# Residual kept in the output, four of eight quads by seven products, one ordinary quad's low parts made by a transfer

## The chip, the cores and the metric

The kernel runs on one core of one Trainium2 chip. The time is the device time of one execution in microseconds; the times shown are medians of several runs. A core has TensorE (PE, matrix products, results in PSUM), VectorE (DVE), ScalarE (ACT), GpSimd (POOL) and SyncE (SP), which here only issues transfers. Each engine works through its own list of instructions in order and waits on semaphores for the others; a transfer is issued by an engine's queue and moved by the core's 16 DMA engines.

## The reference

One transformer layer for 256 tokens of width 2048 in float32. The first half mixes tokens by two attention branches and ends in a projection that is added to the residual x. The second half, where the change lies, is a gated feed-forward network with 5632 hidden columns:

```python
x = x + (g[:, :, 0] * y_a + g[:, :, 1] * y_b) @ w_o
gt, up = jnp.split(rms_norm(x, g_ffn) @ w_gate_up, 2, axis=-1)
return x + (jax.nn.silu(gt) * up) @ w_down
```

## The kernel before, in words

**Three products for one.** float32 operands are split into a high part (rounded to the type fp32r, by ScalarE) and a low part (the operand minus the high part, by VectorE). A product is then three matmuls into the same PSUM bank, high x high, high x low, low x high (`mm3`, L427 to L429). So every weight that is loaded passes through ScalarE (`split_pair`, L220, "wh") and VectorE (L221, "wl") before TensorE can use it.

**The feed-forward stage.** The hidden columns come in 11 blocks of 512, grouped in five parts of 3, 2, 2, 2 and 2 blocks (`PARTS`). For each block there is a gate-up group, which makes 512 columns of gate and 512 of up over all 16 slices of 128 rows of the normalised x. When the blocks of a part are done, their down projection follows, four groups of 512 output columns, two and two interleaved, in chunks of four slices. `evac_down` (L701) then adds a group's PSUM result to the residual `x1[j]` in SBUF on VectorE (L703); after the last part the sum goes out.

**Quads.** A gate-up group consists of eight quads (`Quad`), each a 2 x 2 block product: two token halves, two row slices, gate and up. An ordinary quad does it in 8 block products, 24 matmuls. The quads in `FAST` use a scheme of seven products (21 matmuls), which needs sums of weight blocks: `split_fast` (L837) splits three raw blocks (rh and rl for two, r for one), makes four sums in place in the loaded tile x with four dependent VectorE additions (L844 to L847), and `split` (L850) then splits the four results (wh, wl). The activations get such sums too (`job_h`: hP for an ordinary quad, hs/hsh/hsl for one in `FAST`), once. Ordinary quads add into banks C and D, those in `FAST` into A and B first, then into C and D; `evac_fast` (L658) and `evac_pair` combine the banks on VectorE and ScalarE after the group, and its result is transposed during the next group (tile hid).

**Order and buffers.** SyncE issues the loads; a load needs one of three tiles x (pool `xp`), which is released by the last split that reads it. wh and wl lie in a pool of six (three chunks), the raw parts and all activations in a pool `tp` of 28 tiles of 4 KB per partition. In the feed-forward stage a scheduler of the framework sets the order on each engine from priorities and its own cost model; the order is fixed when the program is built. Chunks are numbered through the program: 253 to 260 are the eight quads of the first gate-up group of part 1, 261 to 268 those of its second, and the tiles of a chunk bear its number (wl255, x257).

Of the kernel before, what the change touches and what calls it, by code (L numbers as in the profile page):

```python
# [41 lines left out]
NPAIR = KD // 2  # L42
FAST = (2, 4, 6)

# [51 lines left out]
def layer_kernel(ctx: ExitStack, tc: tile.TileContext, a: dict, out: bass.AP):  # L96
# [540 lines left out]
    def evac_wo(j):  # L637
        def evac(ps, step):
# [3 lines left out]
            for t in range(NT):  # L642
                nc.scalar.activation(sq[:, t], x1[j][:, t], AF.Square, accum_out=ss2[:, t, j:j + 1])

            for i in (2 * j, 2 * j + 1):
                hjobs[i] = Job(job_h(i))
                hjobs[i].ready = step + 2
                jobs.append(hjobs[i])
# [52 lines left out]
    def evac_down(half, j):  # L701
        def evac(ps, step):
            nc.vector.tensor_add(x1[j], ps, x1[j])  # L703
            if half == len(PARTS) - 1:
                nc.sync.dma_start(od[:, :, j * 512:(j + 1) * 512], x1[j])
        return evac

    def evac_last(ps, t):
# [109 lines left out]
    early = {}  # L818

    def load(c):  # L820
        g, gi, ks, q = chunks[c]
        t = xt[c] = xp.tile([P, 4, 512], F32, name=f"x{c}", tag="x")
        if q:
            for kk in range(2):
                src = g.w[(2 * q.i + kk) * P:(2 * q.i + kk + 1) * P].rearrange("p (n f) -> p n f", n=2)
                nc.sync.dma_start(t[:, 2 * kk:2 * kk + 2], src[:, :, g.c0:g.c0 + 512])
            return
# [9 lines left out]
    def split_fast(c):  # L837
# [10 lines left out]
        raws[c] = {1: (r[:, 0], r[:, 1]), 3: (rh[:, 0], rl[:, 0]), 2: (rh[:, 1], rl[:, 1])}  # L848

    def split(c):  # L850
        g, gi, ks, q = chunks[c]
        if q and q.fast and c not in raws:
            split_fast(c)
# [5 lines left out]
        if q and q.fast:  # L859
            parts[c] = raws.pop(c) | {m: (h[:, n], l[:, n]) for n, m in enumerate((7, 5, 6, 4))}  # L860
        else:
            parts[c] = (h, l)

# [8 lines left out]
    def products_quad(c):  # L872
        q = chunks[c][3]
        bank, w = held["q"], parts.pop(c)
        if not q.fast:
            h, l = w
            for t, n in ((1, 0), (0, 0), (0, 1), (1, 1)):
                m = PLAIN[t, n]
                for kk in range(2):
                    s = slice(t * P, (t + 1) * P)  # L880
                    mm3(bank[m], hP[q.i][:, 0, kk, s], hP[q.i][:, 1, kk, s], h[:, 2 * kk + n], l[:, 2 * kk + n],
                        q.first and kk == 0, q.last and kk == 1)
# [60 lines left out]
    for j in range(4):  # L943
        at(gidx("evac_g0", j), lambda j=j: load_bias(j))
        at(gidx("evac_g1", j), lambda j=j: load_bias(4 + j))
        at(gidx("evac_wo", j), lambda j=j: load_xres(j))

    after_evac = {}
    after_evac[gidx("evac_b", 0)] = lambda: jobs.append(prep["kr"])
# [10 lines left out]
    def splits(to):  # L960

        while ahead["split"] < min(to, n):
            c = ahead["split"]
            loads(c + 1)
            if c + 1 < n and chunks[c + 1][3] and chunks[c + 1][3].fast and c + 1 not in raws:
                loads(c + 2)
                split_fast(c + 1)
            split(c)
            ahead["split"] += 1
# [90 lines left out]
```

## Time and profile before

| | |
|---|---|
| median of 3 runs | 1356.28 us (1355.2 to 1356.44) |
| profiled execution, its own time | 1356.11 us |
| its span in the trace | 1354.3 us |
| TensorE busy | 1339.5 us (99%), clock granted 1.0 |
| VectorE, ScalarE, GpSimd busy | 949.1, 652.2, 34.3 us |
| moved by DMA | 257.14 MB, mean 190 GB/s |
| GpSimd's queue | 224 packets, 0.01 MB |

The page's busy share is an average over stages with different work, so it is read together with the stretches of one gate-up group or one down projection. A row of the timeline has the start, the duration, the engine, the line, the operation with its output and inputs, and in brackets the idle time before it and what ended that. Matmuls overlap: their rate is the distance from start to start.

### The profile page before, as it was taken

The page shows a single profiled execution, that of the slowest core. Times are in us where ns is not written, and L with a number is a line of the kernel's source. Part 1 is how long each engine was busy: PE and PEld are TensorE (multiplying, and loading weights), DVE is VectorE, ACT ScalarE, POOL GpSimd, SP SyncE. Part 2 cuts the span into 40 slices and gives each one's busy share as a digit, 9 for nine tenths or more (in the row PEclk, how much of TensorE's full clock was granted, in tenths as well). Part 3 has the DMA queues.
Part 4 walks back from the last instruction along what each step waited for, and adds up shares of the span by engine and source line. Part 5 has one row for each costly group of instructions (what it writes and reads, how often), then busy time and mean ns, then how long its engine had stood idle before and what let it go on. Part 6 is the DMA issues. An engine that isn't in the chain of part 4 may idle for free.

```text
span 1354.3 us, 16169 instructions
## 1 busy us (share of the span) xinstructions
PE 1339.5 (99%) x6243; PEld 1126.0 (83%) x6243; DVE 949.1 (70%) x949; ACT 652.2 (48%) x724; POOL 34.3 (3%) x41
## 2 busy tenths in 40 slices
PE   8999999999999999999999999999999999999998
PEld 6899999988888888888788888888878888888886
DVE  5566777677645655567789756886798579857973
ACT  6455555454444444455455434454445345534541
POOL 1011112000000000000000000000000000000000
PEclk9999999999999999999999999999999999999999
DMA  7555555656556766676546665565457654754662
GB/s 247 179 175 161 161 170 167 184 161 176 174 186 205 212 188 202 209 235 207 201 158 213 221 187 183 191 213 190 157 185 245 191 186 172 229 190 163 214 214 93
DMA packets 138205, 257.14 MB, mean 190 GB/s; under 512 B 9192, under 2 KB 28688, under 8 KB 138128
## 3 DMA queue, kind: packets, MB, share of 16 engines
q1 hardware_dynamic: 137760, 255.96, 58.9%
q8 instruction: 49, 0.80, 0.2%
q14 instruction: 28, 0.23, 0.1%
q10 hardware_dynamic: 144, 0.13, 0.0%
q0 software_dynamic: 224, 0.01, 0.0%
HBM read 253.97 MB, written 2.10 MB: 189 GB/s over the span
## 4 chain that ended last, share of the span: by engine, by line
PE 94%; DVE 2%; issue 1%; DMA 1%; ACT 1%; SPq 0%; DVEq 0%; ACTq 0%
PE g L429 14%; PE g L427 14%; PE g L428 13%; PE sC L427 6%; PE sC L429 6%; PE sC L428 6%; PE mA L427 4%; PE mA L429 4%; PE mA L428 4%; PE sD L429 4%; PE sD L427 4%; PE sD L428 4%; PE mB L428 3%; PE mB L429 3%; PE mB L427 3%
## 5 line engine op out<-in xcount | busy, mean ns | idle before, releaser
L220 ACT CAST wh<-x 128x1024 fp32r<-128x1024 f32 (+3 forms) x349 | 465.3, 1352 | 437.0 <-DVE x L847 127.7
L221 DVE TENSOR_TENSOR wl<-x,wh 128x2048 fp32r<-128x2048 f32 x132 | 300.8, 2289 | 134.5 <-ACT wh L220 132.7
L221 DVE TENSOR_TENSOR wh<-x,wh 128x1024 fp32r<-128x1024 f32 (+2 forms) x217 | 250.6, 1172 | 113.1 <-ACT wh L220 111.9
L427 PE MATMUL g<-wh,xTh 128*128 128x512 f32 (+1 forms) x544 | 210.6, 387 | 0.6 <-ACT xTh L212 0.6
L429 PE MATMUL g<-wh,xTl 128*128 128x512 f32 (+1 forms) x544 | 207.9, 382 | 0.6 <-DVE xTl L217 0.6
L428 PE MATMUL g<-wh,xTh 128*128 128x512 f32 (+1 forms) x544 | 207.9, 382 | 0.0
L429 PEld LDWEIGHTS g<-wh,xTl 128*128 128x128 f32 x544 | 102.8, 189 | 17.6 <-DVE xTl L217 1.4
L427 PEld LDWEIGHTS g<-wh,xTh 128*128 128x128 f32 x544 | 102.8, 189 | 15.9 <-ACT xTh L212 0.9
L428 PEld LDWEIGHTS g<-wh,xTh 128*128 128x128 f32 x544 | 102.9, 189 | 15.4 <-DVE wh L221 0.4
L427 PE MATMUL sC<-wh,hP 128*128 128x512 f32 x220 | 86.1, 391 | 1.6 <-DVE u L679 1.5
L429 PE MATMUL sC<-wh,hP 128*128 128x512 f32 x220 | 85.7, 390 | 0.0
L429 PE MATMUL sD<-wh,hP 128*128 128x512 f32 x220 | 85.7, 389 | 0.0
L428 PE MATMUL sC<-wl,hP 128*128 128x512 f32 x220 | 85.7, 389 | 0.0
L427 PE MATMUL sD<-wh,hP 128*128 128x512 f32 x220 | 85.7, 389 | 0.0
L428 PE MATMUL sD<-wl,hP 128*128 128x512 f32 x220 | 85.7, 389 | 0.0
L220 ACT CAST rh<-x 128x1024 fp32r<-128x1024 f32 x33 | 34.7, 1051 | 36.1 <-DMA x<-in_w_gate_up_dram 36.1
L427 PEld LDWEIGHTS sC<-wh,hP 128*128 128x128 f32 x220 | 41.3, 188 | 12.3 <-issue 4.0
L427 PE MATMUL g<-wh,mTh 128*128 128x512 f32 x128 | 50.5, 394 | 0.0
L429 PE MATMUL g<-wh,mTl 128*128 128x512 f32 x128 | 49.9, 390 | 0.0
L428 PE MATMUL g<-wh,mTh 128*128 128x512 f32 x128 | 49.9, 390 | 0.0
L427 PEld LDWEIGHTS sD<-wh,hP 128*128 128x128 f32 x220 | 41.3, 188 | 8.6
L428 PEld LDWEIGHTS sD<-wl,hP 128*128 128x128 f32 x220 | 41.3, 188 | 8.6
(675 smaller groups left out, 2390.7 us busy)
## 6 DMA issues: line engine op xcount, KB each, us to landing
x<-in_w_gate_up_dram SPq DMA_DIRECT2D x176, 512.0 KB, 4.7
x<-in_w_down_dram SPq DMA_DIRECT2D x88, 512.0 KB, 5.0
x<-in_w_in_dram SPq DMA_DIRECT2D x79, 512.0 KB, 4.2
x<-in_w_in_dram SPq DMA_DIRECT2D x56, 448.0 KB, 3.6
x<-in_w_o_dram SPq DMA_DIRECT2D x32, 512.0 KB, 4.4
x<-in_w_o_mla_dram SPq DMA_DIRECT2D x16, 512.0 KB, 4.9
x<-in_w_o_dil_dram SPq DMA_DIRECT2D x16, 512.0 KB, 4.6
x<-in_w_ukv_dram SPq DMA_DIRECT2D x8, 512.0 KB, 4.0
```

Source lines behind the costliest of these rows:

```text
L220: nc.scalar.copy(h, x)
L221: nc.vector.tensor_sub(l, x, f32(h))
L427: nc.tensor.matmul(ps, ah, bh, start=first, stop=False)
L428: nc.tensor.matmul(ps, ah, bl, start=False, stop=False)
L429: nc.tensor.matmul(ps, al, bh, start=False, stop=last)
```

## The change

There are three edits.

1. `FAST` becomes (2, 4, 5, 6): quad 5 of each of the 11 gate-up groups is done with seven products.
2. Quad 3 (`BY_DMA`) stays an ordinary quad, but its low parts are no longer made by VectorE. ScalarE writes minus the rounded weights into l and the rounded weights into h, and GpSimd's queue loads the same weights from memory once more with an adding transfer, so that l becomes weight minus high part (`split_by_dma`). This is called two chunks ahead (`EARLY`) and uses four tiles of `tp` in place of a wh and a wl.
3. The residual is written to the output when it is made, and its SBUF tiles are free from then on. After each part but the last ScalarE copies the PSUM result to a tile y and GpSimd's queue adds it to the output in memory; for the last part the output is loaded back (`load_x1`) and the sum is made as before.

```diff
--- before.py
+++ after.py
@@ -40,7 +40,9 @@
 PARTS = ((0, 3), (3, 5), (5, 7), (7, 9), (9, 11))
 PRIO = 200
 NPAIR = KD // 2
-FAST = (2, 4, 6)
+FAST = (2, 4, 5, 6, )
+BY_DMA = (3,)
+EARLY = 2
 
 
 class Job:
@@ -642,6 +644,7 @@
             for t in range(NT):
                 nc.scalar.activation(sq[:, t], x1[j][:, t], AF.Square, accum_out=ss2[:, t, j:j + 1])
 
+            nc.sync.dma_start(od[:, :, j * 512:(j + 1) * 512], x1[j])
             for i in (2 * j, 2 * j + 1):
                 hjobs[i] = Job(job_h(i))
                 hjobs[i].ready = step + 2
@@ -700,10 +703,19 @@
 
     def evac_down(half, j):
         def evac(ps, step):
-            nc.vector.tensor_add(x1[j], ps, x1[j])
-            if half == len(PARTS) - 1:
-                nc.sync.dma_start(od[:, :, j * 512:(j + 1) * 512], x1[j])
+            cols = od[:, :, j * 512:(j + 1) * 512]
+            if half < len(PARTS) - 1:
+                y = t4([P, NT, 512], f"y{half}_{j}")
+                nc.scalar.copy(y, ps)
+                nc.gpsimd.dma_start(cols, y, accum_op=ALU.add)
+            else:
+                nc.vector.tensor_add(x1[j], ps, x1[j])
+                nc.sync.dma_start(cols, x1[j])
         return evac
+
+    def load_x1(j):
+        x1[j] = t4([P, NT, 512], f"x1b_{j}")
+        nc.sync.dma_start(x1[j], od[:, :, j * 512:(j + 1) * 512])
 
     def evac_last(ps, t):
         for c in range(t + 1):
@@ -817,13 +829,17 @@
         first_step.setdefault(chunks[c][1], i)
     early = {}
 
+    def quad_src(c, kk):
+        g, gi, ks, q = chunks[c]
+        src = g.w[(2 * q.i + kk) * P:(2 * q.i + kk + 1) * P].rearrange("p (n f) -> p n f", n=2)
+        return src[:, :, g.c0:g.c0 + 512]
+
     def load(c):
         g, gi, ks, q = chunks[c]
         t = xt[c] = xp.tile([P, 4, 512], F32, name=f"x{c}", tag="x")
         if q:
             for kk in range(2):
-                src = g.w[(2 * q.i + kk) * P:(2 * q.i + kk + 1) * P].rearrange("p (n f) -> p n f", n=2)
-                nc.sync.dma_start(t[:, 2 * kk:2 * kk + 2], src[:, :, g.c0:g.c0 + 512])
+                nc.sync.dma_start(t[:, 2 * kk:2 * kk + 2], quad_src(c, kk))
             return
         if gi == 0 and c:
             load_x(ks[0] * P, (ks[-1] + 1) * P)
@@ -847,8 +863,21 @@
         add(x[:, 3], x[:, 2], x[:, 3])
         raws[c] = {1: (r[:, 0], r[:, 1]), 3: (rh[:, 0], rl[:, 0]), 2: (rh[:, 1], rl[:, 1])}
 
+    def split_by_dma(c):
+
+        x = xt.pop(c)
+        h, l = ([t4([P, 2, 512], f"{n}{k}_{c}", F32R) for k in range(2)] for n in "hl")
+        for k in range(2):
+            nc.scalar.activation(l[k], x[:, 2 * k:2 * k + 2], AF.Copy, scale=-1.0)
+            nc.scalar.copy(h[k], x[:, 2 * k:2 * k + 2])
+            nc.gpsimd.dma_start(l[k], quad_src(c, k), accum_op=ALU.add)
+        parts[c] = [z[k][:, n] for z in (h, l) for k in range(2) for n in range(2)]
+        parts[c] = parts[c][:4], parts[c][4:]
+
     def split(c):
         g, gi, ks, q = chunks[c]
+        if c in parts:
+            return
         if q and q.fast and c not in raws:
             split_fast(c)
         t = xt.pop(c)
@@ -859,7 +888,7 @@
         if q and q.fast:
             parts[c] = raws.pop(c) | {m: (h[:, n], l[:, n]) for n, m in enumerate((7, 5, 6, 4))}
         else:
-            parts[c] = (h, l)
+            parts[c] = ([h[:, n] for n in range(4)], [l[:, n] for n in range(4)]) if q else (h, l)
 
     def needs_of(i):
         c, ks, _, _ = steps[i]
@@ -878,7 +907,7 @@
                 m = PLAIN[t, n]
                 for kk in range(2):
                     s = slice(t * P, (t + 1) * P)
-                    mm3(bank[m], hP[q.i][:, 0, kk, s], hP[q.i][:, 1, kk, s], h[:, 2 * kk + n], l[:, 2 * kk + n],
+                    mm3(bank[m], hP[q.i][:, 0, kk, s], hP[q.i][:, 1, kk, s], h[2 * kk + n], l[2 * kk + n],
                         q.first and kk == 0, q.last and kk == 1)
         else:
             h, l = hq[q.i]
@@ -945,6 +974,9 @@
         at(gidx("evac_g1", j), lambda j=j: load_bias(4 + j))
         at(gidx("evac_wo", j), lambda j=j: load_xres(j))
 
+    for j in range(4):
+        at(gidx("evac_down", 4 * (len(PARTS) - 1) + j), lambda j=j: load_x1(j), 2)
+
     after_evac = {}
     after_evac[gidx("evac_b", 0)] = lambda: jobs.append(prep["kr"])
     after_evac[gidx("evac_b", 6)] = lambda: limited.extend(attn["dil", p] for p in range(4))
@@ -965,6 +997,10 @@
             if c + 1 < n and chunks[c + 1][3] and chunks[c + 1][3].fast and c + 1 not in raws:
                 loads(c + 2)
                 split_fast(c + 1)
+            e = c + EARLY
+            if e < n and chunks[e][3] and chunks[e][3].i in BY_DMA and e not in parts:
+                loads(e + 1)
+                split_by_dma(e)
             split(c)
             ahead["split"] += 1
```

How the scheduler's order changes is shown at three places of part 1. First VectorE in the first group, from the low part of its first quad in `FAST` (255) on. Before:

```order
L221 TENSOR_TENSOR wl255_6410<-x255_6338,wh255_6409 128x2048
L221 TENSOR_TENSOR rl257_6441<-x257_6413,rh257_6440 128x1024
L221 TENSOR_TENSOR r257_6442<-x257_6413,r257_6442 128x512
L221 TENSOR_TENSOR wl256_6452<-x256_6381,wh256_6451 128x2048
L844 TENSOR_TENSOR x257_6413<-x257_6413 128x512
L845 TENSOR_TENSOR x257_6413<-x257_6413 128x512
L846 TENSOR_TENSOR x257_6413<-x257_6413 128x512
L847 TENSOR_TENSOR x257_6413<-x257_6413 128x512
L221 TENSOR_TENSOR wl257_6483<-x257_6413,wh257_6482 128x2048
L221 TENSOR_TENSOR wl258_6522<-x258_6455,wh258_6521 128x2048
L221 TENSOR_TENSOR rl259_6511<-x259_6486,rh259_6510 128x1024
```

And with the change:

```order
L223 TENSOR_TENSOR wl255_6480<-x255_6394,wh255_6479 128x2048
L223 TENSOR_TENSOR rl257_6511<-x257_6483,rh257_6510 128x1024
L223 TENSOR_TENSOR r257_6512<-x257_6483,r257_6512 128x512
L223 TENSOR_TENSOR rl258_6549<-x258_6521,rh258_6548 128x1024
L860 TENSOR_TENSOR x257_6483<-x257_6483 128x512
L223 TENSOR_TENSOR r258_6550<-x258_6521,r258_6550 128x512
L861 TENSOR_TENSOR x257_6483<-x257_6483 128x512
L860 TENSOR_TENSOR x258_6521<-x258_6521 128x512
L862 TENSOR_TENSOR x257_6483<-x257_6483 128x512
L861 TENSOR_TENSOR x258_6521<-x258_6521 128x512
L863 TENSOR_TENSOR x257_6483<-x257_6483 128x512
L862 TENSOR_TENSOR x258_6521<-x258_6521 128x512
```

The raw parts and sums of 257 and 258 (quads 4 and 5) now alternate, and the next rows are rl259, the last sum of 258 and wl257; quad 3 (256) no longer stands in the list.

Second, ScalarE at the same place. Before:

```order
L220 CAST rh255_6366<-x255_6338 128x1024
L220 CAST r255_6368<-x255_6338 128x512
L220 CAST wh254_6377<-x254_6307 128x2048
L220 CAST wh255_6409<-x255_6338 128x2048
L220 CAST rh257_6440<-x257_6413 128x1024
L220 CAST wh256_6451<-x256_6381 128x2048
```

And with the change:

```order
L222 CAST rh255_6424<-x255_6394 128x1024
L222 CAST r255_6426<-x255_6394 128x512
L871 ACTIVATE l0_256_6440<-x256_6435 128x1024
L872 CAST h0_256_6438<-x256_6435 128x1024
L871 ACTIVATE l1_256_6441<-x256_6435 128x1024
L872 CAST h1_256_6439<-x256_6435 128x1024
L709 COPY y0_3_6476<-mA_5135 128x1024
L222 CAST wh255_6479<-x255_6394 128x2048
L222 CAST rh257_6510<-x257_6483 128x1024
L222 CAST r257_6512<-x257_6483 128x512
L222 CAST rh258_6548<-x258_6521 128x1024
L222 CAST r258_6550<-x258_6521 128x512
```

The four operations of quad 3 and a copy of the down projection's result now stand ahead of wh255.

Third, VectorE in the second group, after the low part of its first quad in `FAST` (263). Before:

```order
L221 TENSOR_TENSOR wl263_6697<-x263_6615,wh263_6696 128x2048
L847 TENSOR_TENSOR x265_6700<-x265_6700 128x512
L221 TENSOR_TENSOR wl264_6739<-x264_6661,wh264_6738 128x2048
L215 TENSOR_TENSOR hid1l0_6778<-mA_5115,hid1h0_6777 128x1024
L221 TENSOR_TENSOR wl265_6782<-x265_6700,wh265_6781 128x2048
L221 TENSOR_TENSOR wl266_6821<-x266_6742,wh266_6820 128x2048
L221 TENSOR_TENSOR rl267_6810<-x267_6785,rh267_6809 128x1024
L221 TENSOR_TENSOR r267_6811<-x267_6785,r267_6811 128x512
```

And with the change, a few rows behind wl263 (three sums of 265 stand between):

```order
L217 TENSOR_TENSOR hid1l0_6858<-mA_5135,hid1h0_6857 128x1024
L223 TENSOR_TENSOR rl266_6862<-x266_6822,rh266_6861 128x1024
L223 TENSOR_TENSOR wl265_6873<-x265_6784,wh265_6872 128x2048
L223 TENSOR_TENSOR r266_6863<-x266_6822,r266_6863 128x512
L223 TENSOR_TENSOR rl267_6901<-x267_6876,rh267_6900 128x1024
L860 TENSOR_TENSOR x266_6822<-x266_6822 128x512
L223 TENSOR_TENSOR r267_6902<-x267_6876,r267_6902 128x512
L861 TENSOR_TENSOR x266_6822<-x266_6822 128x512
L860 TENSOR_TENSOR x267_6876<-x267_6876 128x512
L862 TENSOR_TENSOR x266_6822<-x266_6822 128x512
L861 TENSOR_TENSOR x267_6876<-x267_6876 128x512
L863 TENSOR_TENSOR x266_6822<-x266_6822 128x512
```

Two more sums of 267 and then wl266 and wl267 follow. Between wl263 and wl266 there are now two sets of raw parts and their sums. The tile x266 is the one that quad 3 (264) had: its load waits for ScalarE, as SyncE's rows with their waits show (a chunk is two rows; names with HW are earlier loads).

```order
L842 DMA x264_6731<-in_w_gate_up_dram 128x2x512 [waits DMAHW1_49,DMAHW0_49,DVE_49]
L842 DMA x264_6731<-in_w_gate_up_dram 128x2x512
L842 DMA x265_6784<-in_w_gate_up_dram 128x2x512 [waits DMAHW3_49,DMAHW2_49,DVE_49]
L842 DMA x265_6784<-in_w_gate_up_dram 128x2x512
L842 DMA x266_6822<-in_w_gate_up_dram 128x2x512 [waits DMAHW7_49,DMAHW6_49,Activation_49]
L842 DMA x266_6822<-in_w_gate_up_dram 128x2x512
L842 DMA x267_6876<-in_w_gate_up_dram 128x2x512 [waits DMAHW5_49,DMAHW4_49,DVE_49]
L842 DMA x267_6876<-in_w_gate_up_dram 128x2x512
```

The wait on Activation in x266's first row is for the operations of quad 3; the others wait for VectorE.

## Prediction

> **What bounds the kernel now.** I read the page's busy lines first, then the chain that ended last, then the stages one by one.
>
> ```profile
> span 1354.3 us, 16169 instructions
> PE 1339.5 (99%) x6243; PEld 1126.0 (83%) x6243; DVE 949.1 (70%) x949; ACT 652.2 (48%) x724; POOL 34.3 (3%) x41
> PE 94%; DVE 2%; issue 1%; DMA 1%; ACT 1%; SPq 0%; DVEq 0%; ACTq 0%
> ```
>
> TensorE sets the time: it is busy throughout and holds 94% of the chain. A matmul less is time less, if nothing else makes TensorE wait. What a matmul is worth is its distance to the next one, not its 0.39 us, which overlap. Here are the first and last of 18 matmuls in a row of an ordinary quad, and the first of the next group.
>
> ```profile
> 867.91 0.39 PE L427 MATMUL sC<-wh,hP 128*128 128x512 f32 x1
> ...
> 871.77 0.39 PE L429 MATMUL sD<-wh,hP 128*128 128x512 f32 x1
> 872.31 0.47 PE L427 MATMUL sC<-wh,hP 128*128 128x512 f32 x1 [0.16 <-DVE u L679]
> ```
>
> (871.77 - 867.91) / 17 = 0.227 us. An ordinary quad (24 matmuls) takes 5.45 us, one by seven products (21) 4.77 us. The engine that could take TensorE's place is VectorE. Part 1 in three stretches (gate-up group, gate-up group, down; the columns are TensorE, its weight loads, VectorE, ScalarE, GpSimd, each with a count, then clock, DMA share and GB/s):
>
> ```profile
> 829.60:872.30 42.70, 42.56 (x188) 34.94 (x187) 34.89 (x33) 20.16 (x15) 0.00 (x0) 1.00 0.58 197
> 872.30:915.20 42.90, 42.89 (x193) 35.45 (x194) 37.16 (x35) 20.90 (x17) 0.00 (x0) 1.00 0.59 196
> 915.20:959.00 43.80, 42.84 (x194) 35.33 (x193) 27.67 (x21) 19.01 (x13) 0.00 (x0) 1.00 0.59 192
> ```
>
> The 70% of the page is an average: 82% and 87% in the two groups, 63% in the down projection. Waits of TensorE on weights in this part come to one of 0.2 us.
>
> ```profile
> PEld mB L428 <- DVE wl L221: 0.2, 1, 0.2
> ```
>
> **The change part by part.** *TensorE.* Quad 5 of each of 11 groups needs 21 matmuls instead of 24: 33 x 0.227 = 7.5 us less. This is all that the change can win.
>
> *VectorE.* The prices, from the groups of this part:
>
> ```profile
> L221 DVE TENSOR_TENSOR wl<-x,wh 128x2048 fp32r<-128x2048 f32 x25 | 57.0, 2289 | 24.9 <-ACT wh L220 24.8
> L221 DVE TENSOR_TENSOR rl<-x,rh 128x1024 fp32r<-128x1024 f32 x6 | 7.3, 1220 | 1.1 <-ACT rh L220 1.0
> L845 DVE TENSOR_TENSOR x<-x 128x512 f32<-128x512 f32 x6 | 4.1, 691 | 0.2
> L221 DVE TENSOR_TENSOR r<-x,r 128x512 fp32r<-128x512 f32 x6 | 4.1, 684 | 0.0
> L703 DVE TENSOR_TENSOR x<-sC,x x5: 1217/1217/1224, 826.0 to 1338.4; 128x1024 f32<-128x1024 f32 x5
> ```
>
> Quad 5 adds 1.22 + 0.68 + 4 x 0.69 = 4.66 us per group; quad 3's low part, now made by a transfer, takes 2.29 us off. That is +2.4 us in a group that shrinks by 0.7 us: 37.2 + 2.4 = 39.6 of 42.2 us, 94%. The residual adds taken off (16 x 1.22 us) lie in the down stage, where VectorE idles 16 of 43.8 us; there they buy nothing. So VectorE's sum hardly changes, but its peak rises where it was highest.
>
> Does a lead carry it over? In the first group of a part, mostly. Its first quad by seven products is split from T0 + 5.4 us (T0 = 830.4, quad 7's start at 866.56 less the seven quads before it), and the next from 846.91:
>
> ```profile
> 835.84 2.29 DVE L221 TENSOR_TENSOR wl<-x,wh 128x2048 fp32r<-128x2048 f32 x1 [2.06 <-ACT wh L220]
> ...
> 846.91 4.49 DVE L221 TENSOR_TENSOR wl<-x,wh 128x2048 fp32r<-128x2048 f32 x2 [2.05 <-ACT wh L220]
> ```
>
> In the new order ScalarE has four more casts and a copy ahead of that split, so I take 6.1 us. From there the new VectorE order, at the trace's distances from start to start (2.2 us for a low part, 1.14 for rl, 0.6 for r and for adds that alternate, 0.72 for adds in a row), gives the low part of quad 4 at T0 + 19.9, due at 21.8 (three ordinary quads and one by seven, and 0.7 because the first product needs only r); that of quad 6 at 29.9, due at 32.0. No wait.
>
> In the second group it doesn't hold. Now the low part of its quad 2 ends 12.7 us after the group's start (872.3):
>
> ```profile
> 882.75 2.29 DVE L221 TENSOR_TENSOR wl<-x,wh 128x2048 fp32r<-128x2048 f32 x1
> 884.96 0.69 DVE L847 TENSOR_TENSOR x<-x 128x512 f32<-128x512 f32 x1
> 885.56 2.29 DVE L221 TENSOR_TENSOR wl<-x,wh 128x2048 fp32r<-128x2048 f32 x1
> 887.76 1.22 DVE L215 TENSOR_TENSOR hid1l<-mA,hid1h 128x1024 fp32r<-128x1024 f32 x1
> ```
>
> What comes before it is unchanged, so I keep 12.7. The new order then has three adds (2.2), the hidden tile's low part (1.1), rl of quad 5 (1.1), the low part of quad 4 (2.2), r of 5 and rl of 6 (1.7), seven operations of 0.6 (4.2): 25.2 us. Then ScalarE's cast of quad 5 takes 1.9 and its low part 2.2: 29.3 to 29.5. TensorE wants it at 2 x 5.45 + 0.87 (transposes) + 4.77 + 5.45 + 4.77 + 0.7 = 27.5. It waits about 1.9 us. Quad 6's low part follows 2.2 us on, before it is due. Six groups stand like this (two in part 0, one in each other part): 6 x 1.9 = 11.4 us.
>
> *ScalarE.* Quad 3 costs four operations of 128x1024 instead of one cast of 128x2048, about 4 x 1.05 against 1.91 us, and a quad by seven adds 1.7; at 21 of 42.9 us busy the sum is free, the order is costed above. The 16 copies from PSUM stand in the down stage: 1.02 us each by the hidden tile's cast.
>
> ```profile
> 922.62 1.02 ACT L210 CAST hid1h<-sD 128x1024 fp32r<-128x1024 f32 x1 [0.34 <-PE sD L691]
> 933.32 1.92 ACT L220 CAST wh<-x 128x2048 fp32r<-128x2048 f32 x1 [3.48 <-PE mA L428]
> 935.27 2.29 DVE L221 TENSOR_TENSOR wl<-x,wh 128x2048 fp32r<-128x2048 f32 x1 [0.49 <-ACT wh L220]
> ```
>
> Two of four stand ahead of a cast that waits for the same chunk's end. Cast and low part end 4.2 us after that end now, 5.3 then, and the chunk lasts 5.45: nothing, with 0.3 us for each of 8 as the other bound.
>
> *The accumulating transfers.* The trace has none. Nearest rows:
>
> ```profile
> x<-in_w_gate_up_dram SPq DMA_DIRECT2D x176, 512.0 KB, 4.7
> out_dram<-x SPq DMA_DIRECT2D x3, 512.0 KB, 2.8
> gmix_rows<-in_g_mix_dram SPq DMA_DIRECT2D x1, 8.0 KB, 1.7
> grow<-in_g_cq_dram POOLq DMA_DIRECT2D x1, 2.0 KB, 3.2
> grow<-in_g_ffn_dram POOLq DMA_DIRECT2D x1, 8.0 KB, 6.3
> ```
>
> Between 4.7 us (a plain load of that size) and 6.3 + 2 x 4.7 = 15.7 us (the slowest GpSimd row, and both streams one after the other). I take 4.7 + (3.2 - 1.7) = 6.2, as nearest in size and queue. The second half is issued some 4.8 us after the second group's start (r at 1.9, three operations) and due at 16.5; in the first group some 13 us lie between. Hidden at 6.2, late by 4 us at 15.7. The Trainium skill, "DMA: Bandwidth & Descriptors", section "Anatomy of one DMA — SWDGE (gpsimd) path", puts a plain transfer from GpSimd at 2.0 us + bytes / 436e3, so 3.2 us as an estimate; the 2 KB row's 3.2 us already disagrees with it, and by page or row alike the transfer is hidden.
>
> *Loads.* The tile into which quad 5 loads comes free only when ScalarE has read quad 3. From a tile's release to the use of its load is 6.2 us now (885.56 + 2.2 to 893.97):
>
> ```profile
> 893.97 1.05 ACT L220 CAST rh<-x 128x1024 fp32r<-128x1024 f32 x1 [1.37 <-DMA x<-in_w_gate_up_dram]
> ```
>
> In the second group that is 5.9 + 6.2 = 12.1, used by VectorE at 15.9 after 1.1 on ScalarE behind the hidden tile: 2 us to spare. The four stores and four reloads of the residual (2.8 and 4.7 us) lie a chunk or more ahead of any use: nothing.
>
> *Start.* Quad 5's activations now go the seven-product way, and the first group gets one more such quad amid this: 0.5 us.
>
> Sum: -7.5 + 11.4 + 0.5 = +4.4 us on the profiled execution's own 1356.1 us, which lies 0.2 under the median shown: **1360.5 us**.
>
> **The rivals.** *The lead suffices: faster.* VectorE in the two groups waits 12.6 us for ScalarE's casts, eight times; three quads by seven in a row, with their operations alternating, fill such gaps.
>
> ```profile
> DVE wl L221 <- ACT wh L220: 12.6, 8, 2.1
> ```
>
> For it: only 0.2 us of this reaches TensorE now. Against: the 1.9 us above are counted with hardly a gap in them. With 0.5 us of wait a group in place of 1.9, it is -7.5 + 3 = -4.5: 1351.6 us.
>
> *A draw.* With 1.2 us per group the gain is just used up: 1356 us. It needs VectorE some 0.7 us a group earlier than I count.
>
> *The transfers crowd out the loads: much slower.* Quad 3's two accumulating transfers run while the tile of quad 5 is loaded, at a DMA share of 0.58 already. They move 1 MB, and must read the tile too, so a load that shares the engines with them may come 3 us later, half its time again. The first group has 1.9 us to spare at quad 4, the second 2 us in the load and none behind it. From about 2 us of delay on, every microsecond counts in each of 11 groups: 3 us cost about 11 more, 1371 us. The Trainium skill, same page, section "Issuing engines are not separate DMA queues", says that transfers of all issuers interleave on the same 16 engines, which is this rival's premise; no run here shows it, as GpSimd's queue moved only 0.01 MB.
>
> **How the numbers follow.** Forecast (VectorE late in the second groups, 1359 to 1367) 0.38; faster 0.32; draw 0.18; crowded loads or a slow transfer 0.12. The range takes in the lead's full use on one side and the crowded loads on the other, 1349 to 1374; the forecast's own range is 1359 to 1367. A measurement of this kernel tells about 0.2% (2.7 us) from no change: faster 0.32, same 0.18, slower 0.50.
>
> **What would show it.** In the new profile: 33 matmuls fewer at 0.227 us; VectorE at 90% or more in the groups and under 60% in the down stage; TensorE waiting on wl at quad 5 (bank A or B) of the second group, near 2 us, once per group; no wait on l. The forecast is wrong if TensorE's waits on wl stay under 1 us a group (then it is faster), if it waits on a transfer into l, or if ScalarE's rh waits for loads grow by microseconds.

## The result and the profile after

| | before | after |
|---|---|---|
| median of the runs (us) | 1356.53 (1355.2 to 1360.68) | 1403.11 (1400.19 to 1404.82) |
| profiled span (us) | 1354.3 | 1401.5 |
| matmuls | 6243 | 6210 |
| ratio of the times | | 1.0336, 95% interval 1.0319 to 1.0354 |

The change costs 46.6 us; forecast were 4.4, with 1374 us as the range's upper end. One of e15's twelve runs (below) was a slow one, 1914.63 us at a mean granted clock of 0.656, and its ratio leaves that run out. The page of the profile after: span, busy times, the GB and share of the DMA queues (q0 is GpSimd's, with the adding transfers; q1 carries the plain ones), and the chain of work that ended last.

```profile
span 1401.5 us, 16335 instructions
...
PE 1351.4 (96%) x6210; PEld 1127.3 (80%) x6210; DVE 952.0 (68%) x991; ACT 706.4 (50%) x796; POOL 75.5 (5%) x79
...
q1 hardware_dynamic: 139936, 260.15, 57.0%
q0 software_dynamic: 10560, 19.94, 8.8%
...
PE 70%; DMA 11%; DVE 8%; ACT 6%; issue 4%; SPq 1%; DVEq 0%; ACTq 0%
```

The 33 matmuls are gone, VectorE's sum is where it was (952 against 949 us), but TensorE holds 70% of the chain instead of 94%, and DMA 11% instead of 1%. The waits of the kernel after that name the place (us in total, times, longest):

```profile
ACT rh L222 <- DMA x<-in_w_gate_up_dram: 67.6, 23, 6.8
...
PE mA L429 <- ACT wh L222: 18.8, 6, 4.8
...
PE mA L430 <- DVE wl L223: 10.8, 9, 2.0
...
PE sC L429 <- DVE u L682: 3.0, 1, 3.0
```

and the first of them in the kernel before:

```profile
ACT rh L220 <- DMA x<-in_w_gate_up_dram: 36.1, 23, 2.5
```

I listed every distance from one matmul's start to the next in the feed-forward stage. Distances over 0.6 us, each less the normal 0.227, are the "waits" in this text; distances between 0.3 and 0.6 us, each less 0.227, are the "short losses". Two things fall into the short losses: matmuls at half clock, which stand 0.43 us apart, and waits of a tenth or two. Before: 4.8 us of waits and 4.0 of short losses, with a granted clock of 1.00 over the whole stage; after: 42.2 and 20.2, and of the 20.2 some 13 lie where the trace grants a clock of 0.50. With the 7.5 us of the 33 matmuls that is +37.4 + 16.2 - 7.5 = +46.1 of the span's +47.2, and 1.1 us are left over.

Four places hold 27 of the 42 us of waits: quad 4 in the first group of parts 1 to 4. Here is the one of part 2 in the timeline of TensorE (start, duration, and in brackets the wait):

```profile
1000.69 0.39 PE L431 MATMUL mA<-r,hsl 128*128 128x512 f32 x1
1005.92 0.80 PE L429 MATMUL mA<-wh,hsh 128*128 128x512 f32 x1 [4.84 <-ACT wh L222]
1008.48 0.79 PE L430 MATMUL mA<-wl,hsh 128*128 128x512 f32 x1 [1.76 <-DVE wl L223]
1009.07 0.63 PE L431 MATMUL mA<-wh,hsl 128*128 128x512 f32 x1
1009.50 0.63 PE L429 MATMUL mB<-wh,hsh 128*128 128x512 f32 x1
```

The chain of the kernel after says why the cast came late (start, duration):

```profile
980.84 0.94 ACT h L872
...
982.38 14.96 DMA x<-in_w_gate_up_dram
...
997.36 1.06 ACT rh L222
...
998.44 0.04 DVE rl L223
...
1006.14 2.29 DVE wl L223
```

The load of quad 5 starts when ScalarE has read quad 3 out of its tile, as the prediction has it, and takes 15 us instead of 6.2. The split of quad 5 stands on VectorE ahead of the sums of quad 4, so quad 4 waits on quad 5's load. The stretches around it (columns as in the prediction):

```profile
983.00:997.00 14.00, 14.00 (x63) 11.61 (x62) 4.12 (x3) 3.14 (x3) 1.18 (x1) 1.00 1.08 272
997.00:1008.00 11.00, 4.88 (x20) 3.32 (x18) 9.56 (x12) 6.65 (x6) 0.00 (x0) 0.82 0.18 68
1008.00:1014.00 6.00, 5.52 (x13) 4.37 (x14) 5.90 (x7) 0.21 (x1) 0.00 (x0) 0.50 0.69 224
```

For 14 us the DMA engines are full (share 1.08) while VectorE has 4 us of work; in the next 11 us they do almost nothing (0.18), and TensorE is busy for 4.9 of the 11. No load tile is free then: SyncE's own waits between 970 and 1015 show its next load held for up to 18.8 us by the split that frees its tile.

```profile
SPq L842 <- DVE wl L223: 32.4, 5, 18.8
```

The mean DMA share of the two profiles does not show this.

### The profile page after: what moved, and what is told of

Same layout as the page of the kernel before. It is cut to its first block, busy times and chain, and to the rows that moved or that the text cites. A ratio compares the mean times of both kernels' runs of the same rounds, so it can differ in the third digit from the quotient of the medians.

```text
span 1401.5 us, 16335 instructions
## 1 busy us (share of the span) xinstructions
PE 1351.4 (96%) x6210; PEld 1127.3 (80%) x6210; DVE 952.0 (68%) x991; ACT 706.4 (50%) x796; POOL 75.5 (5%) x79
## 3 DMA queue, kind: packets, MB, share of 16 engines
q1 hardware_dynamic: 139936, 260.15, 57.0%
q0 software_dynamic: 10560, 19.94, 8.8%
## 4 chain that ended last, share of the span: by engine, by line
PE 70%; DMA 11%; DVE 8%; ACT 6%; issue 4%; SPq 1%; DVEq 0%; ACTq 0%
PE g L431 12%; PE g L429 12%; PE g L430 12%; DMA x<-in_w_gate_up_dram 9%; PE mA L430 3%; PE mA L431 3%; PE mA L429 3%; PE sC L429 3%; PE sC L430 3%; PE sC L431 3%; PE mB L431 2%; PE mB L430 2%; ACT wh L222 2%; PE mB L429 2%; DMA x<-in_w_o_dram 2%
## 5 line engine op out<-in xcount | busy, mean ns | idle before, releaser
L222 ACT CAST wh<-x 128x1024 fp32r<-128x1024 f32 (+3 forms) x338 | 444.3, 1334 | 380.3 <-DVE x L863 85.3
L223 DVE TENSOR_TENSOR wl<-x,wh 128x2048 fp32r<-128x2048 f32 x121 | 275.4, 2288 | 144.2 <-ACT wh L222 144.2
L223 DVE TENSOR_TENSOR rl<-x,rh 128x1024 fp32r<-128x1024 f32 x44 | 53.6, 1219 | 45.7 <-ACT rh L222 45.7
L222 ACT CAST rh<-x 128x1024 fp32r<-128x1024 f32 x44 | 46.2, 1049 | 67.6 <-DMA x<-in_w_gate_up_dram 67.6
L873 POOL DMA_DIRECT2D l<-in_w_gate_up_dram x22 | 23.9, 1086 | 702.7 <-DVE rl L223 456.8
L429 PE MATMUL sC<-wh,hP 128*128 128x512 f32 x132 | 52.3, 397 | 3.6 <-DVE u L682 3.0
L430 PE MATMUL sC<-wl,hP 128*128 128x512 f32 x132 | 52.0, 394 | 0.0
L431 PE MATMUL sC<-wh,hP 128*128 128x512 f32 x132 | 51.9, 393 | 0.0
L431 PE MATMUL sD<-wh,hP 128*128 128x512 f32 x132 | 51.6, 391 | 0.0
L429 PE MATMUL sD<-wh,hP 128*128 128x512 f32 x132 | 51.5, 390 | 0.0
L430 PE MATMUL sD<-wl,hP 128*128 128x512 f32 x132 | 51.5, 390 | 0.0
L431 PE MATMUL g<-wh,mTl 128*128 128x512 f32 x128 | 49.9, 390 | 0.0
L710 POOL DMA_DIRECT2D out_dram<-y x16 | 19.2, 1199 | 337.5 <-ACT y L709 337.5
```

Source lines behind the costliest of these rows:

```text
L222: nc.scalar.copy(h, x)
L223: nc.vector.tensor_sub(l, x, f32(h))
L429: nc.tensor.matmul(ps, ah, bh, start=first, stop=False)
L430: nc.tensor.matmul(ps, ah, bl, start=False, stop=False)
L431: nc.tensor.matmul(ps, al, bh, start=False, stop=last)
L710: nc.gpsimd.dma_start(cols, y, accum_op=ALU.add)
```

## The experiments

All ratios are against runs of the kernel before on the same chip in the same set of experiments. The six sets ran on different chips, and the kernel before has medians from 1356.5 to 1360.0 us in them, so a difference of times between two sets is good to some 3 us, and the ratios are firmer. "Waits" and "short losses" are as above; in the profiles of e15, e20, e21, e22 and e23 no part of the stage has half the clock, so their last column is short waits alone.

| run | time (us) | ratio, 95% interval | waits | short losses |
|---|---|---|---|---|
| the change | 1403.11 | 1.0336 (1.0319 to 1.0354) | 42.2 | 20.2 |
| e1 small output adds | 1385.74 | 1.0207 (1.0183 to 1.0230) | 29.1 | 15.4 |
| e2 small low-part adds | 1368.89 | 1.0079 (1.0055 to 1.0103) | 19.2 | 9.1 |
| e3 both small | 1355.01 | 0.9976 (0.9966 to 0.9987) | 8.2 | 6.7 |
| e4 low part plain | 1382.39 | 1.0176 (1.0149 to 1.0203) | 25.9 | 17.2 |
| e6 residual only | 1370.72 | 1.0081 (1.0054 to 1.0108) | 16.1 | 8.6 |
| e7 VectorE makes low parts | 1377.83 | 1.0144 (1.0121 to 1.0167) | 26.0 | 12.5 |
| e8 residual in SBUF | 1399.68 | 1.0298 (1.0276 to 1.0320) | 39.1 | 18.5 |
| e9 as e8, quad 7 | 1410.57 | 1.0380 (1.0343 to 1.0416) | 47.6 | 18.3 |
| e13 fourth quad alone | 1370.54 | 1.0095 (1.0081 to 1.0110) | 19.9 | 9.2 |
| e15 fourth quad in 5 groups | 1358.03 | 1.0003 (0.9991 to 1.0015) | 6.4 | 6.1 |
| e16 three quads, low part | 1425.24 | 1.0504 (1.0477 to 1.0530) | 58.9 | 24.1 |
| e17 as e7, small output adds | 1372.64 | 1.0114 (1.0096 to 1.0132) | 21.3 | 10.0 |
| e18 change, four load tiles | 1377.01 | 1.0144 (1.0129 to 1.0159) | 27.5 | 10.7 |
| e19 as e16, small adds | 1381.08 | 1.0173 (1.0156 to 1.0190) | 25.0 | 10.5 |
| e20 as e7, four load tiles | 1363.41 | 1.0045 (1.0030 to 1.0060) | 18.3 | 5.4 |
| e21 as e13, four load tiles | 1350.45 | 0.9940 (0.9927 to 0.9952) | 7.8 | 3.0 |
| e22 as e15, four load tiles | 1352.83 | 0.9957 (0.9944 to 0.9971) | 4.9 | 3.5 |
| e23 before, four load tiles | 1352.39 | 0.9955 (0.9943 to 0.9968) | 3.7 | 1.7 |

### Bytes or order: e1 to e4

These four have every engine's rows in the change's order; only the bytes of transfers differ.

```diff
 e1, e3
-                nc.gpsimd.dma_start(cols, y, accum_op=ALU.add)
+                nc.gpsimd.dma_start(cols[:, :, :8], y[:, :, :8], accum_op=ALU.add)
 e2, e3
-            nc.gpsimd.dma_start(l[k], quad_src(c, k), accum_op=ALU.add)
+            nc.gpsimd.dma_start(l[k][:, :, :8], quad_src(c, k)[:, :, :8], accum_op=ALU.add)
 e4
-            nc.gpsimd.dma_start(l[k], quad_src(c, k), accum_op=ALU.add)
+            nc.gpsimd.dma_start(l[k], quad_src(c, k))
```

> The adds into the output move 8 of 512 columns only (so most of the residual sum of parts 0 to 3 is left out); every engine's order is as in the changed kernel. Theory A (crowding: the adding transfers hold the DMA engines while quad 5 of the first group of a part is loaded, and VectorE and ScalarE have this load's split ahead of quad 4's sums): two of the four adding transfers in that place are gone, some 6 us of the engines' time, so that load lands after 8 to 10 us instead of 14, the wait before quad 4 falls from 7.3 to under 3.5 us, time 1366 to 1382 us. Theory B (order: three quads by seven in a row are late on VectorE whatever is transferred): no change, 1395 to 1405 us.

> The transfers into l add 8 of 512 columns only (so quad 3's low parts are wrong for the rest, and the result with them); orders unchanged. A: 6.5 us of the engines' time leave the same place and the second group's, the load of quad 5 lands after 7 to 9 us in the first group and 6 in the second, time 1360 to 1374 us. B: 1395 to 1405 us.

> Both kinds of adding transfer reduced to 8 columns (the same parts of the sum left out as in the two runs before); orders unchanged. A: the load lands after 6 us as in the kernel before, no wait before quad 4 over 1 us, and what is left is the forecast's own term, quad 5 late by about 2 us in the second groups: 1352 to 1362 us. B: 1395 to 1405 us.

> The transfers into l move all their bytes but overwrite instead of adding (quad 3's low parts are then the weights themselves); orders unchanged. If adding costs a second pass of the engines (the reading of the tile), 3.2 us of their time leave: the load lands after 10 to 12 us, 1383 to 1396 us. If the bytes from GpSimd's queue cost twice as much for another reason: unchanged within 4 us of 1403.

The output's bytes are worth 17 us of the change's time and the low part's 34; together 48. The order alone, with its 33 matmuls less, gives 1355: by its ratio it wins some 3 us, of the 7.5 that the matmuls are worth. So it is the bytes, and the order is not what loses. e3 at the place shown above (ScalarE and VectorE in the timeline, part 2):

```profile
967.23 1.04 ACT L872 CAST h<-x 128x1024 fp32r<-128x1024 f32 x1
...
973.74 1.05 ACT L222 CAST rh<-x 128x1024 fp32r<-128x1024 f32 x1 [1.22 <-DMA x<-in_w_gate_up_dram]
```

From the tile's release (968.27) to the cast 5.5 us; in the change 981.77 to 997.36, 15.6 us. With small transfers the load takes what the prediction assumed, and TensorE never waits there. The time from release to cast falls step by step as bytes go: in the first groups of parts 1 to 4 it is 14.6 to 15.6 us in the change, 12.4 to 13.1 in e4, 10.5 to 11.8 in e1, 8.1 to 10.9 in e2 and 5.5 to 5.9 in e3, in the order of the five times.

e4 moves all the bytes but doesn't add. From the queue and issue rows of e4:

```profile
q0 software_dynamic: 10560, 19.94, 7.1%
...
l<-in_w_gate_up_dram POOLq DMA_DIRECT2D x22, 512.0 KB, 6.3
```

against 8.8% and 8.2 us in the change:

```profile
l<-in_w_gate_up_dram POOLq DMA_DIRECT2D x22, 512.0 KB, 8.2
out_dram<-y POOLq DMA_DIRECT2D x16, 512.0 KB, 6.6
```

Not adding is worth 21 of the 34 us, so both the volume and the adding itself count. e2 and e3 came out where crowding alone was expected to put them; e1 came out some 4 us above its expectation and e4 just under the lower edge of its own.

### One part at a time: e6, e7, e8, e13, e17

```diff
 e6 (three quads by seven, no low-part transfer, residual in the output)
-FAST = (2, 4, 5, 6, )
-BY_DMA = (3,)
+FAST = (2, 4, 6)
+BY_DMA = ()
 e7 (four quads, VectorE makes quad 3's low part), e17: and the output adds as in e1
-BY_DMA = (3,)
+BY_DMA = ()
 e8 (residual in SBUF as before, the rest as the change), e13: and BY_DMA = ()
...
-                y = t4([P, NT, 512], f"y{half}_{j}")
-                nc.scalar.copy(y, ps)
-                nc.gpsimd.dma_start(cols, y, accum_op=ALU.add)
...
+            nc.vector.tensor_add(x1[j], ps, x1[j])
...
```

In e8 and what builds on it, the early store of the residual and its load back in the last part go too, as in the kernel before.

> Three quads by seven and VectorE's low parts as before; only the residual goes into the output, by sixteen adding transfers. If adding bytes cost by themselves, as the two small-transfer runs let it be read (removing the output's bytes won 13.9 to 17.4 us with four quads by seven): 1364 to 1374 us. If they cost only because four quads by seven and the low-part transfers leave loads and VectorE no lead: within 3 us of before, 1353 to 1360 us.

> Four quads by seven, VectorE makes the low part of quad 3 too, the residual in the output as in the change. VectorE's groups then hold 37.2 + 4.7 = 41.9 us of work in 42.2. If the transfers into the low part are the main loss and VectorE could have done it: under the run with small low-part transfers or equal to it, 1362 to 1372 us. If VectorE becomes the bound (my late low parts, now 2.3 us more per group): 4 us or more per group in most groups, 1385 to 1415 us, with TensorE's waits on wl, and loads that arrive in time.

> The residual stays in SBUF, added by VectorE, as before; four quads by seven and the two transfers into the low part of quad 3 as in the change. Crowding adds up by bytes: the same as the run with small output transfers, 1380 to 1390 us, since VectorE's 16 adds lie in the down projection where it idles. If VectorE's adds there delay the first group's splits, more: over 1395 us.

> The fourth quad by seven alone: no adding transfer at all, residual added by VectorE in SBUF, VectorE makes every low part. If the added transfers are the whole loss and VectorE could carry it: 1349 to 1358 us. If VectorE's order is what binds (its adds of the down projection stand ahead of the splits of the next group, as the run with the residual in SBUF suggests, and the groups hold 42 us of work in 42): 1368 to 1395 us, with waits on wl and loads that arrive in time.

> As the run in which VectorE makes all low parts, with the output's adding transfers cut to 8 of 512 columns (the residual is then left out but for these columns): VectorE's load alone, its 16 adds in the down projection gone, no adding bytes to speak of. If the output's adds cost some 14 us here too: 1359 to 1367 us. If VectorE is what that run waits for, and not loads: 1372 to 1378 us.

The residual alone costs 11 us (e6), near the 14 that its bytes cost from e3 to e2. The fourth quad alone, with no adding transfer at all, costs 13 us (e13) where it should win 7. Both e13 and e7 are faster than the change: the transfer that was to relieve VectorE costs more than VectorE's 2.29 us per group.

For e13 (and e17) I had VectorE's 42 us of work per group as the cause, with loads in time, and the times fell into that span. The loads are not in time, though. ScalarE waited for them longer than in the change (67.6 us above), which proves little alone, since that row is 49.9 in e23 below, where TensorE waits least of all:

```profile
ACT rh L222 <- DMA x<-in_w_gate_up_dram: 74.1, 34, 5.8
...
PE sC L429 <- DVE u L682: 8.7, 4, 2.7
...
PE mA L430 <- DVE wl L223: 4.7, 8, 1.2
```

The chain of e13 across the boundary of two groups in part 2, where TensorE stands until 1011.12, says more:

```profile
992.23 2.30 DVE wl L223
...
995.13 4.74 DMA x<-in_w_gate_up_dram
...
999.97 1.93 ACT wh L222
...
1001.92 2.29 DVE wl L223
...
1010.29 0.68 DVE u L682
```

A load starts when VectorE's split has freed its tile, the next split waits for that load, and the group's last sums stand behind that split. Followed back 22 us, 13 of the 16 waits that e13 has ahead of its last one have such a load in their chain; but in the 10 us before each of the 16, VectorE is busy for 8.8 to 9.9. So late loads and a full VectorE meet here, and e13's rows don't separate them.

e7 fell between its two expectations. e17 tells what its 16 output adds are worth there, 4 to 5 us. e17 against e13 (1372.6 and 1370.5) also answers the residual's other half: taking the 16 adds off VectorE gains nothing, as predicted. e8 ought to have been near e1 and lies 14 us above it, in the span of its second expectation (VectorE's adds delay the first group's splits). Its VectorE runs the sums of quads 4 and 5 in another order than e1, so two things differ there, and I can't say which share is whose.

### Another place: e9, and three quads by seven: e16, e19

```diff
 e9 (as e8)
-BY_DMA = (3,)
+BY_DMA = (7,)
 e16 (as e8), e19: and the low-part adds as in e2
-FAST = (2, 4, 5, 6, )
+FAST = (2, 4, 6)
```

> As the run with the residual in SBUF, but the low part of quad 7 instead of quad 3 is made by the two transfers. If what counts is that the transfers fall together with the load that the first of three quads in a row by seven needs: most of the loss goes, 1350 to 1368 us, and quad 5's load lands in about 6 us again. If what counts is the engines' time as such, or any load that shares with an adding transfer stalls TensorE: 1378 to 1392 us. VectorE then makes quad 3's low part right ahead of the three quads by seven, so if its lead is what is short: waits on wl at quads 4 to 6, 1370 to 1395 us, with loads in time.

> Before plus the low part of quad 3 by the two adding transfers: three quads by seven, residual in SBUF. VectorE has 2.3 us a group less than before. If adding transfers stall TensorE through the loads by themselves: 1366 to 1385 us. If they only do it where four quads by seven leave the loads no lead: 1352 to 1361 us.

> The run of three quads by seven with the low-part transfers, these cut to 8 of 512 columns (the low part is then wrong but for these), every engine's order the same. If the bytes of the transfers make its loss too: 1350 to 1362 us. If the order (the split of the next group's first quad by seven, which waits for its load, ahead of this group's last sums on VectorE) loses time by itself: 1385 us or more, with the waits of 5 to 8 us on u at the groups' boundary still there.

Both went worse than either expectation. e9 moves the stall rather than removing it; its waits show loads late at other quads, the group's last sums late, and even the cast for the transfer itself waiting for its load:

```profile
ACT rh L222 <- DMA x<-in_w_gate_up_dram: 73.2, 36, 5.5
...
PE sC L429 <- DVE u L682: 22.4, 6, 5.1
...
ACT l L871 <- DMA x<-in_w_gate_up_dram: 20.1, 8, 4.7
```

So the trouble is not that one load. e16 has fewer quads by seven, hence more slack on VectorE, and is the slowest of all. A stretch of e16 before a group's boundary and the one across it:

```profile
890.00:898.00 8.00, 8.00 (x37) 6.64 (x36) 4.48 (x4) 2.70 (x4) 0.00 (x0) 1.00 0.98 369
898.00:906.00 8.00, 2.39 (x7) 1.67 (x7) 8.00 (x12) 6.42 (x8) 2.14 (x2) 0.82 0.46 75
```

No adding transfer runs in the first (GpSimd issues nothing), yet the engines are full with loads: they were held back, came together, and then the group's last sums on VectorE stood behind a split whose load was late (TensorE's waits on u in e16, then in e19):

```profile
PE sC L429 <- DVE u L682: 27.6, 5, 7.4
```

```profile
PE sC L429 <- DVE u L682: 16.0, 5, 3.9
```

With small transfers the same order takes 1381: 44 us are the bytes, and about 24 are what is left, this order and ScalarE's added operations. e19 lies between its two expectations: the order does lose by itself, but its waits on u are at most 3.9 us where 5 to 8 were expected.

### Lead of the loads: e18, e20, e15, e21 to e23

```diff
 e18 (the change), e20 (e7), e21 (e13), e22 (e15), e23 (the kernel before)
-    xp = ctx.enter_context(tc.tile_pool(name="xp", bufs=3))
-    wp = ctx.enter_context(tc.tile_pool(name="wp", bufs=6))
+    xp = ctx.enter_context(tc.tile_pool(name="xp", bufs=4))
+    wp = ctx.enter_context(tc.tile_pool(name="wp", bufs=5))
 e15 (as e13, quad 5 by seven only in a part's last group; its activations are made both ways)
-FAST = (2, 4, 5, 6, )
+FAST = (2, 4, 6)
+MORE = (5,)
+BY_DMA = ()
...
+        fast = sorted(FAST + MORE) if group.more else FAST
+        self.group, self.i, self.fast = group, i, i in fast
...
+        if i in FAST + MORE:
...
+            groups[-1].more = i == len(js) - 1
```

A load tile and a split tile have the same size, so this trades one split tile for a load tile. Every byte and operation stays, but not their order: VectorE's list of operations stands differently at 232 of 991 places in e18 against the change, at 275 of 1018 in e21 against e13, and at 277 of 949 in e23 against the kernel before, and TensorE's and ScalarE's lists differ too. These runs show what the exchange is worth. How much of it is the loads' lead and how much the new order stays open.

> The change with four load tiles and five split tiles (of the same size) in place of three and six; every byte and every operation as in the change. If the loss comes because the load of quad 5 waits for its tile and then shares the DMA engines with the adding transfers: it is issued about a quad (5 us) earlier, lands in time though it takes as long, and the waits of 7 us at quad 4 of parts 1 to 4 fall under 2: 1358 to 1375 us. If the bytes as such are too many at that place, or a split tile less delays the splits: 1392 to 1410 us.

> VectorE makes all low parts, residual in the output, four load tiles and five split tiles. Against the same with three and six (1377.8 us): if loads were part of its loss, 1358 to 1370 us; if VectorE's 42 us of work per group bind, 1372 to 1385 us; the lost split tile can make it worse.

The change gets 26 us back and ends 2 us above the range of my first expectation. Its waits at quad 4 of the first groups stay at 5 to 6 us, where I had expected under 2 (27 us in all become 22); the other waits fall from 15 to 5 us. The load there is still late, in the chain of e18 and its stretch:

```profile
830.36 0.94 ACT h L872
...
831.30 0.46 SPq L842
...
831.81 13.16 DMA x<-in_w_gate_up_dram
```

```profile
838.00:844.00 6.00, 6.00 (x28) 4.99 (x27) 1.55 (x2) 0.00 (x0) 0.00 (x0) 1.00 1.09 261
...
850.00:856.00 6.00, 0.86 (x3) 0.19 (x1) 6.00 (x8) 4.24 (x3) 0.00 (x0) 0.84 0.01 3
```

At that place the two transfers into the low part and the output adds of the down projection's last two column blocks are issued between 824.5 and 833.7, together with the loads. And the load got no lead there, against what I had expected: with four tiles it still takes the one that ScalarE's last read of quad 3 frees (830.36 to 831.30, as in the change). In the first groups its last half is issued 4.2 to 4.6 us after the group's start, in the change 3.9 to 4.1. So e18 does not test what an earlier load of quad 5 would do. It shows that with the same late start the load still takes 13 us beside these bytes, and that the exchange wins at the other places; the load of quad 7, say, which took some 30 us from release to use, takes 11.8.

e20 makes the same exchange without the transfers into the low part: against e7 it wins 14 us (1377.83 to 1363.41), as expected for loads.

> Quad 5 by seven only in the last group of each part (5 of 11), no adding transfer, residual in SBUF, VectorE makes every low part. In the run with VectorE making all low parts the second groups of parts 1 to 4 have no wait over 0.6 us of TensorE, the first groups do. If the first group's start behind the down projection is the place where lead is missing: 15 x 0.227 = 3.4 us less, less 1 for quad 5's activations, which are made both ways: 0.996 to 1.000 of before, 1352 to 1357 us. If VectorE's sum in a group binds wherever it reaches 42 of 42 us: 2 us or more per such group, 1362 to 1372 us.

> Four quads by seven, no adding transfer, residual in SBUF, VectorE makes all low parts, four load tiles and five split tiles. With three and six it was 1370.5 us. If loads in time were what was missing there too: 1350 to 1358 us. If VectorE's 42 us per group bind: 1362 to 1372 us.

> Quad 5 by seven only in the last group of each part, no adding transfer, residual in SBUF, four load tiles and five split tiles. With three and six it was 1358.0 us, no difference from before. If the loads cost the rest (waits of 0.6 to 1.4 us at the groups' boundaries): 1351 to 1355 us, 0.995 to 0.998 of before. If not: 1356 to 1360 us.

> The kernel before with four load tiles and five split tiles, nothing else. TensorE waits for little there (gaps over 0.6 us sum to 4.8 us), so the tiles can win 3 us at most: 1352 to 1357 us. If a split tile less delays the casts: 1358 to 1364 us.

Without adding transfers the exchange more than makes up for the loss. e21 does all that the change computes, with four quads by seven in all groups, and is 0.6% faster than the kernel before. Its page and waits:

```profile
span 1348.7 us, 16239 instructions
```

```profile
ACT rh L222 <- DMA x<-in_w_gate_up_dram: 27.0, 22, 3.2
...
PE sC L429 <- DVE u L682: 4.5, 5, 1.7
```

VectorE does the same work as in e13 (busy for 991.9 and 995.6 us), and TensorE's waits fall from 19.9 to 7.8 us: 42 us of work per group do not bind by themselves. The loads of quad 5 in the first groups are issued 3.7 to 4.3 us after the group's start instead of 8.9 to 9.7. This fits that e13 lacked loads in time, but the order differs too, so it is not shown alone. But most of the gain is the exchange's. The kernel before with it (e23) is 0.45% faster, 6.0 us in its set, where I had allowed 3 at most; the fourth quad adds 1352.39 - 1350.45 = 1.9 us of its 7.5, since 7.8 + 3.0 us of waits and short losses stand against 3.7 + 1.7 there. The intervals of e21 and e23 overlap, so this last step is measured less firmly than either against before. e22 gains nothing over e23. e15 without the tile makes no difference.

## Why the prediction was wrong

**Held.** 33 matmuls of 0.227 us less. VectorE's sum unchanged. Taking the residual's adds off VectorE buys nothing (e13, e17). The transfer into the low part itself is hidden: no wait of TensorE on l, though it lands after 8.2 us where I took 6.2, inside my bounds of 4.7 to 15.7. The tile's release, the point from which quad 5's load counts, was where I put it.

**The load of quad 5 stays at 6.2 us: the step that failed.** It took 14.6 to 15.6 us from release to use at the first groups of parts 1 to 4, and 5.5 to 5.9 in e3, without the bytes. The rival of crowded loads had the mechanism, and the Trainium skill's "Issuing engines are not separate DMA queues" ("DMA: Bandwidth & Descriptors"), on which it leaned, agrees with this: 15.6 us for the load beside GpSimd's transfers, 5.5 without their bytes. Its price was far too small, for three reasons. It put 3 us on a load where 9.4 came. It counted the two low-part transfers alone; the output's adding transfers, which I priced at nothing but ScalarE's copies, fall into the same 15 us of the first groups and are worth 17 us by e1. And while it did name that the transfers read the tile as well, its 3 us is what 1 MB takes at the plain rate (3.2 us at 326 GB/s); at the 162 GB/s of the adding ones it is 6.5 (below). Its sign did appear: ScalarE's wait for loads grew from 36.1 to 67.6 us. I also had the groups the wrong way round: I saw no slack in the second group and 2 us in the first, but the first is where the down projection's adds meet the loads. The range ended at 1374 because of this price.

**"It waits about 1.9 us. Six groups": 11.4 us that aren't there.** e3 has the change's order without the bytes, and TensorE's waits on wl sum to 0.4 us. VectorE in it is as late as I worked out, or nearly: the low part of quad 5 in part 2's second group ends 28.4 us after the group's start at 1006.72, where I had 29.3 to 29.5.

```profile
1032.85 2.29 DVE L223 TENSOR_TENSOR wl<-x,wh 128x2048 fp32r<-128x2048 f32 x1 [0.65 <-ACT wh L222]
```

(A slip beside this: the due time of 32.0 for quad 6 in a first group counts quad 5 as an ordinary quad; it is 31.4, and still no wait follows.) What I had wrong is when TensorE wants it. I allowed 0.7 us from the quad's start to the first product with wl; in the timeline of e3's TensorE it is 1035.88 - 1033.61 = 2.3 us: ten products that need no wl stand ahead there, not three. The group's first row and the quad's:

```profile
1006.72 0.47 PE L429 MATMUL sC<-wh,hP 128*128 128x512 f32 x1
...
1033.61 0.39 PE L429 MATMUL mA<-r,hsh 128*128 128x512 f32 x1
...
1034.29 0.39 PE L429 MATMUL mA<-wh,hsh 128*128 128x512 f32 x1
1034.52 0.39 PE L429 MATMUL mB<-wh,hsh 128*128 128x512 f32 x1
...
1035.88 0.39 PE L430 MATMUL mA<-wl,hsh 128*128 128x512 f32 x1
```

I had read VectorE's rows in the new order and assumed TensorE's. So the sign came out right for a reason that was not there.

**The clock.** No term of the sum had it, and 13 of the 46 us are matmuls at half clock, all behind waits (last section); waits too short to count as such make 3 more.

## What to carry to other kernels

A mean DMA share of 0.6 says nothing about room for more transfers: look at the share in the stretch where the new bytes fall, and at when a tile comes free for the next load, because full engines followed by idle ones can mean a lack of load tiles (here a load stood 18.8 us for a tile). Before moving work from a compute engine to the DMA engines, cost its bytes as time on the engines that the critical loads use, adding ones at their own rate (here 162 GB/s against 326), and add up all transfers of the change that meet in one place. And when a kernel sits close to its bound, a load buffer more may be worth more than the arithmetic saved: here the exchange won 6.0 us and the 33 matmuls 1.9, though what the new order did in the 6.0 is not known.

## What the runs showed of the hardware

**Adding transfers are dear on the engines.** In the change, 19.94 MB of q0 take 8.8% of 1401.5 = 123 us of all 16 engines, 162 GB/s; the plain 260.15 MB take 57.0%, 799 us, 326 GB/s. In e4, where 11.5 of the 19.94 MB are copied instead of added, q0 takes 7.1% of 1381.7 = 98 us: 25 us less for these 11.5 MB.

**The clock falls after a wait.** In the last of the stretches shown of the kernel after, the granted clock is 0.50, and the matmuls at 1009.07 and 1009.50 stand 0.43 us apart instead of 0.227. Over the profiles of all twenty kernels, with waits taken together that begin within 8 us of the first, I added up the short losses in these 8 us. At 132 places with under 2 us of waits the median is 0.1 us. At 47 places with 2 to 3 us it is at most 0.3 us in 24 of them and 1.5 to 1.7 in the other 23. At 44 places with 3 us or more the median is 2.0 us, the most 2.9. So the loss comes in pieces of some 1.7 us or hardly at all; the stretches at half clock in the change's stage last 3.41 us (two), 6.83 (two) and 10.24 (two). A long wait so costs more than it lasts, and many short ones of the same sum cost less: in the change 13 us at half clock stand beside 42 of waits, in e20 none beside 18. The Trainium skill ("TensorE: Matmul & The Clock Gate", section "Part 1: The HAM clock gate (the "warmup" mystery)") has the halved clock after at least one idle window of about 3.4 us, and 426.7 ns from start to start of such matmuls. The pitch agrees. The window does not: in the change a single wait of 2.0 us, at 705.54, was followed by 1.65 us of slow matmuls.
